# Scaling the residual rows on GpSimd in the up stages instead of the down stages, and two modulation vectors computed in the retention stage

## The chip, the core and the metric

One core of one Trainium2 chip runs the whole program. TensorE (PE) multiplies, VectorE (DVE), ScalarE (ACT) and GpSimd (POOL) do elementwise work, and the queue of SyncE (SP) issues most DMAs. Each engine works through its own instructions strictly in order and waits on semaphores for the others. The metric is device microseconds of one execution, taken as the median of several runs.

## The reference

Two layers, each a mixer and a convolutional feed-forward network (FFN), on 1024 rows of 1024 features in float32. The mixer of layer 0 is a gated delta net, that of layer 1 is retention. Cut to what the change touches:

```python
e = silu(c @ cond_w + cond_b)
for i in range(2):
    mod = e @ ada_w[i] + ada_b[i]
    sh1, sc1, g1, sh2, sc2, g2 = split(mod, 6)
    y = mixer[i](x * (1 + sc1) + sh1)
    x = layer_norm(ALPHA * x + (1 + g1) * y, ln_g[i, 0], ln_b[i, 0])
    y = conv_ffn(x * (1 + sc2) + sh2, ...)      # silu(conv(gate)) * up, then @ w_down
    x = layer_norm(ALPHA * x + (1 + g2) * y, ln_g[i, 1], ln_b[i, 1])
```

The six vectors of `mod` are numbered 0 to 5: groups 0 and 1 are `sh1` and `sc1`, 3 and 4 are `sh2` and `sc2`.

## The kernel before

**Matrix products.** The float32 operands are split in a rounded part and the rest (`split`, L88: ACT copies at L89, DVE subtracts at L90), and each product is three matmuls. The big products use a fast scheme with seven block products instead of eight. In `strassen` a function `wino(n, sink)` (L1207) handles item n: it loads two weight tiles `wa` and `wb` (1024 columns each, four blocks a11, a12, a21, a22; tag `wr`, two buffers, so the loads of an item wait until the item before has used its own), and computes seven products of 12 matmuls. Their left sides are a11, a12, and the sums s1, s2, s4, s3 that `psub` (L1204) has DVE write into PSUM tiles of the tag `mm` (two buffers), and a22. PE takes them in the order a11, a12, s1 (on T1), s2 (on T2), s4 (on 22), and then a22 (on T4) and s3 (on T3). `block` splits each left side into tiles `wb` first.

**Stages.** Layer 0: mixer, then the up product (22 items, two by two: an item for the convolved gate, an item for the up half; the results are stored in `ad`), then the down product (`proj_gen`). Layer 1: retention projections through `strassen` with 16 items, where items 0 and 1 and 10 to 15 make gates and items 2 to 9 are rope items (`rope_item`, L1610, with rotations on DVE and POOL), then the retention core, the output product, up and down as before. Items 0 and 1 of a `strassen` call are handled apart, `wino` takes the rest.

**Residual rows.** The layer norm that ends a mixer leaves rows without the gain and bias of the norm in `xs0` (layer 0) and `xs2` (layer 1). The down stage needs them with both, as float32 rows of the residual. `proj_gen` has POOL do this: `gain_half` (L1335) loads a 128x512 piece of rows 512 to 1023 into a `lane` tile, multiplies and adds (L1341), and stores it to `xg` (L1342) in the first two of the seven products; `xload` (L1344) loads rows 0 to 511 in the third product and scales them in place (L1349). Gain and bias are broadcast to all partitions by `gain_rows` into four tiles of the tag `auh` (eight buffers).

**Modulation vectors.** `bg_ada(i, j, kind)` queues eight units for one group of `mod`: each loads 512 KB of `ada_w` into a tile `mvw` (tag `lane`, four buffers, inside `strassen`) and has DVE multiply and add twice (L214, L216). The fourth and the eighth unit of a group also have PE transpose the 128x512 sum into an `mm` tile (L226), ACT sum it by rows (L228), and DVE add the bias (L230, L232). `wino` calls `bg_step` twice per item, and each call runs the next unit: once after the product on 22, once at the end of the item. The `mm` tile of the transposes thus comes from the same two buffers as the sums of `psub`.

**Order.** A scheduler turns the program's order into one order per engine; it may move an instruction ahead of others that it holds to be ready later.

Of the kernel before, what the change touches and what calls it, by code (L numbers as in the profile page):

```python
# [12 lines left out]
ALU = mybir.AluOpType  # L13
AX = mybir.AxisListType

P = 128
# [3 lines left out]
HALF = 512  # L20
# [13 lines left out]
def trunk_kernel(ctx: ExitStack, tc, A):  # L34
# [330 lines left out]
    def gain_rows(n, key, tag="auh"):  # L365
        return [row_load(A[nm][n:n + 1, :], key, sp, tag) for nm in ("ln_g", "ln_b")]
# [782 lines left out]
        dve.tensor_tensor(b, a, b, ALU.add)  # L1149
        return b  # L1150

    def strassen(hT0, xts, scale, shift, items, tags=("hTb", "hTb", "qkv", "qkv", "aux"), direct=False):
        B = {"11": hT0[:4], "21": hT0[4:]}
        nblk = [0]
        nacc = [0]

        def mm_on(*a, **kw):
            return pe.matmul(*a, skip_group_check=True, **kw)  # L1158
# [24 lines left out]

        def block(src):
            n = nblk[0]
            nblk[0] += 1
            t = tl(("wh", "wl")[n % 2], [P, 2, HALF], F32R, name="wb")
            split(t[:, 0], t[:, 1], src)
            return kn(t[:, 0]), kn(t[:, 1])

        def prod(src, b, onto=None):
            w = block(src)
            if onto is None:
                nacc[0] += 1
                acc = (acc_tile, acc_tile, sc_tile)[nacc[0] % 3]()
            else:
                acc = onto
            for k in range(4):
                mm3(acc, w, k, B[b][k], onto is None and k == 0, k == 3, mm_on if onto is not None else pe.matmul)
            return acc  # L1200

        def psub(x, y, op=ALU.subtract):
            t = mm_tile()
            dve.tensor_tensor(t, x, y, op)  # L1204
            return t

        def wino(n, sink):  # L1207
            ua, ub = items[n][:2]
            wa, wb = tl("wr", [P, D]), tl("wr", [P, D])
            sp.dma_start(wa, ua)  # L1210
            sp.dma_start(wb, ub)
            a11, a12, a21, a22 = wa[:, hs(0)], wa[:, hs(1)], wb[:, hs(0)], wb[:, hs(1)]
            def copy_of(X, tag="cv"):
                t = tl(tag, [P, 516] if tag == "cv" else [P, HALF], name="pc")[:, 0:HALF]
                act.activation(t, X, AF.Copy)  # L1215
                return t
# [12 lines left out]
            prod(s4, "22", Z)  # L1229
            sink(1, Z, u2)  # L1230
            bg_step()
            prod(s3, "T3", X)
            u3 = copy_of(X, "t2")
            sink(3, X, z5)
            sink(2, prod(a22, "T4"), u3)
            bg_step()

        bg_tag[0] = "lane"
        for n in range(2):
            if not direct:  # L1240
                sinks.append(items[n][2]())
                for i in range(2):
                    sinks[n](2 * i, ahead[n][i], None)
            X = side(n, 1)
            for i in range(2):
                sinks[n](2 * i + 1, X[i], None)
            if n == 0:
                rest()
            if items[n][3]:
                items[n][3]()  # L1250
        for n in range(2, len(items)):
            wino(n, items[n][2]())
            if items[n][3]:
                items[n][3]()
        bg_tag[0] = "wr"
        return B
# [5 lines left out]
            return raw  # L1262
        return ablk

    def proj_gen(nj, ablk, wsrc, slots, xsrc, G, final, ln_next, tag, ltags, dst, key, mm=pe.matmul, gate=None, gain=None):
# [64 lines left out]

        xts = [[], []]
        stats = [[], []]
        grows = gain_rows(gain[0], key) if gain else None

        def gain_half(n):  # L1335
            hf, rs = n // 4, slice(HALF + n % 4 * P, HALF + (n % 4 + 1) * P)
            x = tl("lane", [P, HALF], name="xg")
            with after("w"):
                sp.dma_start(x, gain[1][rs, hs(hf)])
            for r, op in zip(grows, (ALU.mult, ALU.add)):  # L1340
                pool.tensor_tensor(x, x, r[hf], op)  # L1341
            pool.dma_start(xsrc[rs, hs(hf)], x)  # L1342

        def xload(half, t):  # L1344
            xt = load_row(xsrc if half or not gain else gain[1], half, t)
            if half == 0 and gain:
                for r, op in zip(grows, (ALU.mult, ALU.add)):
                    for hf in range(2):
                        pool.tensor_tensor(xt[:, hs(hf)], xt[:, hs(hf)], r[hf], op)  # L1349
            xts[half].append(xt)  # L1350
            stats[half].append(tl("st", [P, 2, 6]))

        def finish(half, t, nh, c):
# [74 lines left out]
        for p, (an, bn, fin) in enumerate(prods):  # L1428
# [3 lines left out]
            for j in range(nj):  # L1432
                if gate and p < 2:
                    yield gate(j)
                    yield from take("qkv", 2)
                    give("qkv", 2)
                a, w = ops(an, bn, j, not gate and p < (7 if final else 5))
                with after("a"):
                    for st in steps[p * nj + j + ahead:p * nj + j + ahead + 1]:
                        load_b(*st)  # L1440
                if gain and p < 2 and j % 2 == 0 and p * 4 + j // 2 < 8 and j < 8:
                    gain_half(p * 4 + j // 2)
                if gain and p == 2 and j % 2 == 0 and j < 8:
                    xload(0, j // 2)
                if p == 2 and j < 4 and gate:
                    xload(0, j)
                    finish(0, j, 0, c11[j])
                if j >= nj - depth:
                    tail.append((j, a, w))
                else:  # L1450
                    for t in range(4):
                        mma(accs[t], t, a, w, j == 0, False, mm if p < 2 else pe.matmul)
                        yield 0.0
                if p == 5 and j > 1:
                    for _ in range(-(-16 // (nj - 2))):
                        if hooks:
                            hooks.pop(0)()
                bg_step()
# [27 lines left out]
    def layer_tail(i, mix, wout, xsrc, x_mid, x_out, ln_next, final):  # L1486
# [13 lines left out]
            hT0, xts = proj_st(mix[0])  # L1500
        bg_ada(i, 5, "row")
        if i == 0:
            for j in (1, 0, 4, 3):
                bg_ada(1, j, "col")
        cw = vcol(f"ffn_conv{i}")
        cb = vcol(f"ffn_convb{i}")
        ad = dr.tile([NF // 2, 7, P, HALF], F32, tag=f"ad{i}", name=f"ad{i}")
        up = A["ffn_up"][i]

        def pair_items(fp):  # L1510
            g, o = [], []
# [30 lines left out]
            def up_start():  # L1542
                seen = []

                def gated(q, a, b):
# [7 lines left out]
                    if len(seen) == 4:  # L1553
# [8 lines left out]
        strassen(hT0, xts, sc2, sh2, [it for fp in range(NF // 2) for it in pair_items(fp)])  # L1562
        slots = {"c": "hTa", "x": "qkv"}
        gb2 = gain_rows(3, ("mid", i), "hTb") if final else None
        return proj_st(proj_gen(NF // 2, ablk_of(ad, "qkv"), A["ffn_down"][i], slots, xg[i + 1], rows[i, 5],
                       (gb2, x_out) if final else None, ln_next, "hTb", ("hTb", "hTa", 8, 6, "f") if final else ("qkv", "hTa", 8, 4, "0"), x_out, ("out", i), gain=(2 * i, x_mid)))

    g1 = two("auh", F32, "g1")
    for nh in range(2):
# [64 lines left out]
    def gate_item(u):  # L1634
        def start():
            def sink(q, a, b):
# [4 lines left out]
        return A["ret_wg"][u], A["ret_wg"][u + 1], start, None  # L1641

    sc_r, sh_r = next0()
    B = strassen(h0, xts, sc_r, sh_r, [gate_item(0), gate_item(2)]
                 + [rope_item(h, j) for h in range(RH) for j in range(2)] + [gate_item(u) for u in range(4, 16, 2)], ("hTa", "aux", "qkv", "qkv", "hTa"), True)
    hT = [h0, []]
# [275 lines left out]
```

## Time and profile before

| | before |
|---|---|
| median of 3 runs | 3039.41 us (3034.10 to 3042.13) |
| profiled execution | 3032.61 us, of which its instructions span 3030.8 us |
| mean granted TensorE clock | 0.971 |
| up stage of layer 0, about | 840 to 1205 us of the span |
| down stage of layer 0, about | 1205 to 1480 us |
| rope items of retention, about | 1528 to 1690 us |
| up stage of layer 1, about | 2440 to 2790 us |
| down stage of layer 1, about | 2790 to 3030 us |
| POOL, L1341 (rows 512 to 1023) | 32 instructions, median 1629 ns, longest 17768 ns |
| SP loads at L210 (`ada_w`) | 80, median 4.3 us from issue to landing |

The trace is read by its views: the busy time of each engine in chosen stretches (with the granted clock of PE), the list of which engine waited for which, and the instructions in order of time. A row in order of time holds the start, the duration, engine, line, operation, output and input, size, and in brackets how long the engine had been idle and for what. Two rows that start 0.60 us apart and last 0.68 us overlap in the pipeline; the distance of the starts is then the cost of one. Consecutive matmuls overlap likewise.

### The profile page before, as it was taken

Reading aid. Unit: us, or ns where it says so; the run is one execution under the profiler, and the core shown is the slowest. Engines: PE = TensorE matmul, PEld = TensorE weight load, DVE = VectorE, ACT = ScalarE, POOL = GpSimd, SP = SyncE. Lnnn points to the kernel's source line nnn. Section 1 sums busy time; section 2 is a strip of 40 time slices with the busy share of each in tenths; the row PEclk is TensorE's granted clock in tenths of the full one; section 3 lists DMA queues with packets and bytes.
Section 4 is the critical chain, followed back from the end, with each engine's and each line's share of the span. In section 5 each row is a group of like instructions: output and inputs, shape, how many; then the busy total and the mean of one; then the engine's idle time right before and its main releaser. Section 6 shows DMA issues by size and latency. Waiting matters only on the chain. (4 is left out here: it accounts for less than half of the span.)

```text
span 3030.8 us, 38796 instructions
## 1 busy us (share of the span) xinstructions
PE 2840.2 (94%) x13590; PEld 2312.4 (76%) x13590; DVE 2271.4 (75%) x3841; ACT 1316.8 (43%) x2408; POOL 672.8 (22%) x629
## 2 busy tenths in 40 slices
PE   8889998999999999998999999999999899999997
PEld 7768876887778788786777787767777678888785
DVE  5785786545888888998788645566688887778988
ACT  4655555434544445445432442222243544445442
POOL 0410311033021111730023303422200011113704
PEclk9999998999999999999999999999998999999998
DMA  7222221354344545854322444666663332336663
GB/s 271 89 70 74 98 82 62 116 170 138 106 153 151 158 158 182 309 193 141 126 105 98 166 160 144 200 184 186 202 217 132 98 136 104 105 105 227 232 188 108
DMA packets 243027, 450.22 MB, mean 149 GB/s; under 512 B 22928, under 2 KB 76432, under 8 KB 242832
## 3 DMA queue, kind: packets, MB, share of 16 engines
q1 hardware_dynamic: 211648, 400.02, 40.0%
q10 hardware_dynamic: 29760, 43.00, 3.9%
q0 software_dynamic: 1424, 4.72, 0.4%
q8 instruction: 107, 1.75, 0.2%
q14 instruction: 88, 0.72, 0.1%
HBM read 339.13 MB, written 108.53 MB: 148 GB/s over the span
## 5 line engine op out<-in xcount | busy, mean ns | idle before, releaser
L636 PE MATMUL acc<-hT,wh 128*128 128x512 f32 x960 | 302.8, 397 | 0.0
L1556 POOL TENSOR_TENSOR o<-o 128x512 f32<-128x512 f32 x88 | 121.1, 1386 | 725.4 <-DVE o L1549 622.9
L279 PE MATMUL acc<-bb,ab 128*128 128x512 f32 x504 | 205.5, 408 | 18.8 <-DVE bb L90 18.7
L1158 PE MATMUL acc<-T,wb 128*128 128x512 f32 x840 | 205.3, 393 | 8.7 <-DVE wb L90 8.6
L636 PEld LDWEIGHTS acc<-hT,wh 128*128 128x128 f32 x960 | 184.3, 192 | 34.5
L278 PE MATMUL acc<-bb,ab 128*128 128x512 f32 x504 | 192.2, 407 | 16.9 <-DVE ab L90 10.3
L636 PE MATMUL acc<-hT,wl 128*128 128x512 f32 x480 | 204.3, 426 | 0.3 <-ACT sg L1084 0.3
L89 ACT ACTIVATE ab<-ar 128x512 fp32r<-128x512 f32 x210 | 129.8, 624 | 168.6 <-PE acc L280 87.9
L280 PE MATMUL acc<-bb,ab 128*128 128x512 f32 x504 | 202.6, 403 | 0.0
L1158 PEld LDWEIGHTS acc<-T,wb 128*128 128x128 f32 x840 | 157.9, 189 | 46.1 <-DVE wb L90 12.4
L90 DVE TENSOR_TENSOR wb<-wr,wb 128x512 fp32r<-128x512 f32 x162 | 116.0, 718 | 92.8 <-ACT wb L89 89.5
L90 DVE TENSOR_TENSOR ab<-ar,ab 128x512 fp32r<-128x512 f32 x210 | 169.2, 812 | 15.1 <-ACT ab L89 14.7
L90 DVE TENSOR_TENSOR wl<-wr,wh 128x1024 fp32r<-128x1024 f32 x85 | 106.4, 1252 | 89.7 <-ACT wh L89 89.7
L90 DVE TENSOR_TENSOR wb<-mm,wb 128x512 fp32r<-128x512 f32 x216 | 145.1, 683 | 22.8 <-ACT wb L89 20.9
L89 ACT ACTIVATE wh<-wr 128x1024 fp32r<-128x1024 f32 x101 | 106.8, 1058 | 121.3 <-PE acc L636 56.1
L89 ACT ACTIVATE wb<-mm 128x512 fp32r<-128x512 f32 x216 | 122.8, 593 | 72.5 <-DVE mm L1204 72.4
L1215 ACT ACTIVATE pc<-acc 128x512 f32<-128x512 f32 x143 | 84.5, 593 | 154.0 <-PE acc L1158 95.2
L636 PE MATMUL acc<-wh,hT 128*128 128x512 f32 x384 | 138.0, 422 | 2.0 <-DVE vv L90 2.0
L89 ACT ACTIVATE wb<-wr 128x512 fp32r<-128x512 f32 x162 | 99.3, 627 | 92.2 <-DMA wr<-in_ffn_up 45.9
L1535 DVE SCALAR_TENSOR_TENSOR o<-g,vc,o 128x512 f32<-128x512 f32 (+2 forms) x176 | 138.2, 804 | 0.8 <-ACT o L1530 0.2
L457 DVE SCALAR_TENSOR_TENSOR qkv<-raw,vc,qkv 128x512 f32<-128x512 f32 x144 | 114.6, 800 | 30.4 <-ACT qkv L455 29.3
L279 PEld LDWEIGHTS acc<-bb,ab 128*128 128x128 f32 x504 | 98.9, 196 | 44.7 <-DVE bb L90 24.3
(634 smaller groups left out, 7792.0 us busy)
## 6 DMA issues: line engine op xcount, KB each, us to landing
wr<-in_ffn_up SPq DMA_DIRECT2D x96, 512.0 KB, 4.0
mvw<-in_ada_w SPq DMA_DIRECT2D x80, 512.0 KB, 4.3
ad<-o SPq DMA_DIRECT2D x154, 256.0 KB, 2.2
ar<-ad SPq DMA_DIRECT2D x154, 256.0 KB, 4.4
Br<-in_ffn_down SPq DMA_DIRECT2D x88, 256.0 KB, 4.1
wr<-in_ret_wv SPq DMA_DIRECT2D x32, 512.0 KB, 3.7
ar<-od SPq DMA_DIRECT2D x56, 256.0 KB, 5.3
xs<-xt ACTq DMA_DIRECT2D x24, 512.0 KB, 3.8
```

The source lines that it names most:

```text
L89: act.activation(dst_h, src, AF.Copy)
L90: eng.tensor_tensor(dst_l, src, dst_h, ALU.subtract)
L278: mm(acc, a[1][:, sl], w[0], start=first, stop=False)
L279: mm(acc, a[0][:, sl], w[1], start=False, stop=False)
L280: mm(acc, a[0][:, sl], w[0], start=False, stop=last)
L457: dve.scalar_tensor_tensor(oh, raw[:, 3 - j:515 - j], w[:, 3 - j:4 - j], oh, ALU.mult, ALU.add)
L636: pq(pe.matmul(out, lhsT, rhs, start=start, stop=stop), cost)
L1158: return pe.matmul(*a, skip_group_check=True, **kw)
L1215: act.activation(t, X, AF.Copy)
L1535: dve.scalar_tensor_tensor(tv, gv[:, c0 - j:c1 - j], w[:, 2 - j:3 - j], tv, ALU.mult, ALU.add)
L1556: pool.tensor_tensor(o[d], o[x], o[y], op)
```

## The change

`gain_half` and the scaling in `xload` go. A new function `scale_rows` is called by `wino` right after the two weight loads of each item of an up stage. In item 5 it loads gain and bias; in each of items 6 to 21 it loads a 128x512 piece of the rows into an `auh` tile, has POOL multiply and add, and has POOL's queue store it to `xg`. All 1024 rows go that way, so the down stage loads finished rows. The order of the loads is pinned behind the load of `wb` (`anchor["i"]`).

In layer 0's `layer_tail`, groups 4 and 3 of layer 1 are no longer queued beside groups 1 and 0; they are queued ahead of the retention projections. There are two units per item and 16 units, so they fall on items 2 to 9, the rope items.

```diff
@@ wino
-            sp.dma_start(wb, ub)
+            anchor["i"] = sp.dma_start(wb, ub)
+            if beside:
+                beside(n)
@@ proj_gen
-        grows = gain_rows(gain[0], key) if gain else None
-
-        def gain_half(n):
-            hf, rs = n // 4, slice(HALF + n % 4 * P, HALF + (n % 4 + 1) * P)
-            x = tl("lane", [P, HALF], name="xg")
-            with after("w"):
-                sp.dma_start(x, gain[1][rs, hs(hf)])
-            for r, op in zip(grows, (ALU.mult, ALU.add)):
-                pool.tensor_tensor(x, x, r[hf], op)
-            pool.dma_start(xsrc[rs, hs(hf)], x)
-
         def xload(half, t):
-            xt = load_row(xsrc if half or not gain else gain[1], half, t)
-            if half == 0 and gain:
-                for r, op in zip(grows, (ALU.mult, ALU.add)):
-                    for hf in range(2):
-                        pool.tensor_tensor(xt[:, hs(hf)], xt[:, hs(hf)], r[hf], op)
-            xts[half].append(xt)
+            xts[half].append(load_row(xsrc, half, t))
...
-                if gain and p < 2 and j % 2 == 0 and p * 4 + j // 2 < 8 and j < 8:
-                    gain_half(p * 4 + j // 2)
-                if gain and p == 2 and j % 2 == 0 and j < 8:
+                if not gate and p == 2 and j % 2 == 0 and j < 8:
                     xload(0, j // 2)
@@ layer_tail
         if i == 0:
-            for j in (1, 0, 4, 3):
+            for j in (1, 0):
                 bg_ada(1, j, "col")
...
+        grows = []
+
+        def scale_rows(n):
+            if n == 5:
+                grows.extend(gain_rows(2 * i, "i"))
+            if not 6 <= n < 22:
+                return
+            hf, rs = (n - 6) // 8, slice((n - 6) % 8 * P, (n - 6) % 8 * P + P)
+            x = tl("auh", [P, HALF], name="xg")
+            with after("i"):
+                sp.dma_start(x, x_mid[rs, hs(hf)])
+            for w, op in zip(grows, (ALU.mult, ALU.add)):
+                pool.tensor_tensor(x, x, w[hf], op)
+            pool.dma_start(xg[i + 1][rs, hs(hf)], x)
@@ retention projections
     sc_r, sh_r = next0()
+    for j in (4, 3):
+        bg_ada(1, j, "col")
     B = strassen(h0, xts, sc_r, sh_r, ...
```

**POOL at the entry of the first down stage, before.** `o` are the up stage's last sums, `xg` the scaled pieces, `xt` whole rows of the residual.

```order
L1556 TENSOR_TENSOR o<-o 128x512 x40
L1341 TENSOR_TENSOR xg<-xg,rowb 128x512 x5
L1342 DMA xg_170<-xg 128x512 x2
L1341 TENSOR_TENSOR xg<-xg,rowb 128x512
L1342 DMA xg_170<-xg 128x512
L1556 TENSOR_TENSOR o<-o 128x512 x2
```

The same engine in the up stage of the change (its lines from 1211 on are numbered otherwise: L1555 is L1556 of before, L1506 and L1507 are new):

```order
L1555 TENSOR_TENSOR o<-o 128x512 x8
L1506 TENSOR_TENSOR xg<-xg,rowb 128x512 x2
L1507 DMA xg_170<-xg 128x512
L1555 TENSOR_TENSOR o<-o 128x512 x4
L1506 TENSOR_TENSOR xg<-xg,rowb 128x512 x2
L1507 DMA xg_170<-xg 128x512
```

One pair of POOL instructions and one store now stand in each item of the up stage from item 6 on, and the down stage has none.

**DVE at the start of a rope item, before.** `wb` are split halves of a block (L90), `mm` the sums of `psub` (L1204), `pc` and `rm` the values and products of the rotation (L1149, L1622 to L1627). The first row splits a11, the third makes s1, the fourth splits a12, and `wb_13504` is the split of s1.

```order
L90 TENSOR_TENSOR wb_13465<-wr_13461,wb_13465 128x512
L1149 TENSOR_TENSOR pc_13388<-acc_13356,pc_13388 128x512
L1204 TENSOR_TENSOR mm_13483<-wr_13462 128x512
L90 TENSOR_TENSOR wb_13485<-wr_13461,wb_13485 128x512
L1204 TENSOR_TENSOR mm_13502<-mm_13483,wr_13461 128x512
L1624 TENSOR_TENSOR pc_13388<-pc_13388,cosT_13268 128x512
L1149 TENSOR_TENSOR pc_13369<-sc_13317,pc_13369 128x512
L1149 TENSOR_TENSOR pc_13423<-sc_13438,pc_13423 128x512
L90 TENSOR_TENSOR wb_13504<-mm_13483,wb_13504 128x512
```

In the change, at the start of item 6 (items 4, 8 and 10 read alike), a12's split `wb_13754` is followed by eight rotation rows (cosine, two L1149, two products, difference, cosine, sum), and then by these; `ada` and `v14` belong to the modulation group, and `wb_13773` is the split of s1:

```order
L1625 TENSOR_TENSOR pc_13580<-pc_13580,rm_13706 128x512
L216 SCALAR_TENSOR_TENSOR ada_13498<-mvw_13715,e_162,ada_13498 128x512
L1149 TENSOR_TENSOR pc_13750<-acc_13757,pc_13750 128x512
L1626 TENSOR_TENSOR pc_13677<-pc_13677,rm_13706 128x512
L216 SCALAR_TENSOR_TENSOR ada_13498<-mvw_13715,e_162,ada_13498 128x512
L1204 TENSOR_TENSOR mm_13752<-wr_13731 128x512
L230 SCALAR_TENSOR_TENSOR v14_13388<-cs_13720,vc_153 128x4
L1204 TENSOR_TENSOR mm_13771<-mm_13752,wr_13730 128x512
L214 TENSOR_SCALAR ada_13828<-mvw_13829,e_162 128x512
```

Three small rows follow (L251, L252, L216), and then `wb_13773`. Before, s1 was made between the splits of a11 and a12; now it stands behind the whole rotation of the item before and behind the last unit of a modulation group, because that unit's transposes take an `mm` tile ahead of it in the program's order, and the split of s1 stands behind L230 and the first unit of the next group.

**SP in the rope items.** The `wr` are the two weight tiles of an item, the `mvw` the tiles of `ada_w`.

```order
L1210 DMA wr_13400<-in_ret_wqk 128x1024
L1211 DMA wr_13401<-in_ret_wqk 128x1024
L210 DMA mvw_13384<-in_ada_w 128x2x512
L210 DMA mvw_13499<-in_ada_w 128x2x512
L1794 DMA qk_15477<-qd_12622 128x512
```

Before, only `wr` (and now and then `qk`) stood there; two loads of 512 KB have moved in behind each pair of weight tiles. The tag `lane` of `mvw` also holds the products `rm` of the rotation and, all through retention, one table, so that a load of `mvw` can start only when an earlier `rm` or `mvw` is used up.

More of the change, by code (lines that the diff above doesn't have):

```diff
@@ L1150, in c_of, with strassen @@
         return b
-    def strassen(hT0, xts, scale, shift, items, tags=("hTb", "hTb", "qkv", "qkv", "aux"), direct=False):
+    def strassen(hT0, xts, scale, shift, items, tags=("hTb", "hTb", "qkv", "qkv", "aux"), direct=False, beside=None):
         B = {"11": hT0[:4], "21": hT0[4:]}
@@ L1263, in ablk_of, with proj_gen @@
         return ablk
-    def proj_gen(nj, ablk, wsrc, slots, xsrc, G, final, ln_next, tag, ltags, dst, key, mm=pe.matmul, gate=None, gain=None):
+    def proj_gen(nj, ablk, wsrc, slots, xsrc, G, final, ln_next, tag, ltags, dst, key, mm=pe.matmul, gate=None):
         bal = {nm: BAL[ltags[4] + nm] for nm in ABLK + ("w11", "w21", "w22", "wT1", "wT2", "wT3", "wT4", "n", "h")}
@@ L1560, in pair_items @@
             return [(up[4 * fp], up[4 * fp + 2], gate_start, conv), (up[4 * fp + 1], up[4 * fp + 3], up_start, None)]
-        strassen(hT0, xts, sc2, sh2, [it for fp in range(NF // 2) for it in pair_items(fp)])
+        strassen(hT0, xts, sc2, sh2, [it for fp in range(NF // 2) for it in pair_items(fp)], beside=scale_rows)
         slots = {"c": "hTa", "x": "qkv"}
@@ L1565, in layer_tail @@
         return proj_st(proj_gen(NF // 2, ablk_of(ad, "qkv"), A["ffn_down"][i], slots, xg[i + 1], rows[i, 5],
-                       (gb2, x_out) if final else None, ln_next, "hTb", ("hTb", "hTa", 8, 6, "f") if final else ("qkv", "hTa", 8, 4, "0"), x_out, ("out", i), gain=(2 * i, x_mid)))
+                       (gb2, x_out) if final else None, ln_next, "hTb", ("hTb", "hTa", 8, 6, "f") if final else ("qkv", "hTa", 8, 4, "0"), x_out, ("out", i)))
     g1 = two("auh", F32, "g1")
```

## The prediction

> **What bounds the kernel now.** First the totals, then the busy time by stage (stretch, length, busy us of PE, PEld, DVE, ACT and POOL with counts, granted clock, DMA share, GB/s), then the waits of PE (sum, times, longest).
>
> ```profile
> PE 2840.2 (94%) x13590; PEld 2312.4 (76%) x13590; DVE 2271.4 (75%) x3841; ACT 1316.8 (43%) x2408; POOL 672.8 (22%) x629
> ```
>
> PE is busy for 94% of the span and none of its matmuls goes away. So the time can change by PE's waits and by time at a lower granted clock, and by nothing else.
>
> ```profile
> 840.00:1205.00 365.00, 356.33 (x1559) 289.85 (x1559) 302.21 (x475) 167.66 (x331) 53.03 (x40) 1.00 0.48 156
> 1205.00:1410.00 205.00, 195.13 (x846) 158.17 (x845) 190.18 (x261) 99.29 (x180) 82.01 (x48) 0.98 0.70 238
> 1528.00:1690.00 162.00, 150.46 (x642) 121.59 (x642) 135.48 (x178) 48.87 (x85) 55.24 (x34) 0.98 0.32 111
> 2440.00:2790.00 350.00, 350.00 (x1543) 289.11 (x1542) 265.51 (x394) 166.39 (x283) 60.68 (x45) 1.00 0.37 127
> 2790.00:2940.00 150.00, 144.15 (x620) 118.15 (x619) 136.71 (x168) 66.14 (x118) 67.44 (x36) 0.98 0.67 229
> ```
>
> In order: up and the entry of down of layer 0, the rope items, up and the entry of down of layer 1. DVE is the runner-up everywhere: 93% in the first down stage, 91% in the second, 84% in the rope items, 83% and 76% in the up stages. The waits that end last are DVE's too, at the entry of down 0 (1205 to 1300), of down 1 (two rows), and in the rope items (two rows):
>
> ```profile
> PE acc L279 <- DVE bb L90: 5.0, 2, 3.6
> PE acc L279 <- DVE bb L90: 3.0, 1, 3.0
> PE acc L278 <- DVE ab L90: 2.9, 1, 2.9
> PE acc L1158 <- DVE wb L90: 7.5, 5, 2.6
> PE sc L1158 <- DVE wb L90: 4.1, 3, 2.6
> ```
>
> In up 1 no wait of PE is listed at all, as the equal 350.00 of length and PE's busy time says.
>
> **Part 1, the down stages lose their POOL work.** Why DVE is late there:
>
> ```profile
> 2803.60 5.97 DVE L90 TENSOR_TENSOR ab<-ar,ab 128x512 fp32r<-128x512 f32 x1
> 2809.49 0.68 DVE L90 TENSOR_TENSOR bb<-Bw,bb 128x512 fp32r<-128x512 f32 x1
> 2809.71 0.47 PE L278 MATMUL acc<-bb,ab 128*128 128x512 f32 x1 [2.86 <-DVE ab L90]
> ...
> 2841.50 10.99 DVE L1305 TENSOR_TENSOR Bw<-Bw 128x512 f32<-128x512 f32 x1
> 2841.93 10.01 POOL L1349 TENSOR_TENSOR xt<-xt,rowb 128x512 f32<-128x512 f32 x8
> 2853.15 0.50 PE L279 MATMUL acc<-bb,ab 128*128 128x512 f32 x1 [2.96 <-DVE bb L90]
> 2809.70:2814.70 5.00, 4.95 (x14) 3.75 (x15) 5.00 (x9) 0.66 (x2) 0.19 (x1) 0.66 0.95 311
> ```
>
> The same DVE subtract takes 0.68 us or 5.97, and one operation lasts 10.99 while eight POOL instructions (10.01) run beside it; 0.7 us after it ends, one split later, PE goes on. After such a stall the clock is granted at 0.66 for 5 us, which loses 5 x 0.34 = 1.7 us. Without POOL in these stages the four waits of L278 and L279 (5.0 + 3.0 + 2.9 = 10.9) and three such stretches (3 x 1.7 = 5.1) go: **-16**. At least the two long waits of down 1 and their last one's clock go (5.9 + 1.7, about -8); at most, with PE's other idle time in the row of 1205 to 1410 (205 - 195.1 - 5.0 = 4.9), about -21. Late next would be the loads, at 70% of the DMA in these rows; the change moves none of them in, and takes the loads of the pieces out.
>
> **Part 2, two modulation groups among the rope items.** The rows of the order show it: in items 4, 6, 8 and 10 the sum s1 comes after the whole rotation of the item before, after the last unit of a group and its transposes; the split of s1, without which PE can't start T1, also follows L230 and the next group's first unit (not in item 10, the last). PE holds two products then, a11 and a12. The rows for this walk:
>
> ```profile
> 1652.33 0.39 PE L110 MATMUL sc<-hT,wb 128*128 128x512 f32 x1
> 1657.77 0.39 PE L110 MATMUL acc<-T,wb 128*128 128x512 f32 x1
> 1654.90 1.27 DVE L1149 TENSOR_TENSOR pc<-acc,pc 128x512 f32<-128x512 f32 x2
> 1657.45 3.37 POOL L1625 TENSOR_TENSOR pc<-pc,cosT 128x512 f32<-128x512 f32 x2 [3.02 <-DVE rm L1622]
> 1662.50 1.28 DVE L90 TENSOR_TENSOR wb<-mm,wb 128x512 fp32r<-128x512 f32 x2
> 1663.23 4.62 PE L1158 MATMUL sc<-T,wb 128*128 128x512 f32 x12 [2.58 <-DVE wb L90]
> 1663.20:1668.20 5.00, 4.97 (x15) 3.94 (x16) 3.67 (x6) 2.03 (x4) 0.00 (x0) 0.66 0.67 210
> ```
>
> ```profile
> L214 DVE TENSOR_SCALAR ada<-mvw,e x20: 474/486/489, 72.3 to 2450.7; 128x512 f32<-128x512 f32 x20
> L216 DVE SCALAR_TENSOR_TENSOR ada<-mvw,e,ada x140: 710/745/1782, 73.3 to 2472.3; 128x512 f32<-128x512 f32 x140
> 1100.99 0.60 PE L226 MATMUL mm<-cst,ada 128*128 128x128 f32 x4
> 1224.32 0.26 ACT L228 ACTIVATE ada<-mm 128x128 f32<-128x128 f32 x1
> ...
> 1225.22 0.21 ACT L228 ACTIVATION_READ_ACCUMULATOR ada<-mm 128x1 f32 x1
> DMA to landing us min/median/max: 3.7/4.3/7.4
> ```
>
> Two products last 1657.77 - 1652.33 = 5.44 us. Say PE starts a11 at t. The last product of the item before ends at about t as well, and two of the rotation's inputs wait for it. From 1654.90 to 1662.50 DVE runs the eight rotation operations, one split and one sum, in 7.6 us; less 0.6 each for the last two, 6.4. Then two L216 (0.72 each, between the 0.71 and 0.745 of its row), L1149 and L1626 (0.6 each), 2.6: t + 9. Transposes 0.6: t + 9.6. The chain of L228 (1224.32 to 1225.43, four sums) and L230, 1.2: t + 10.8. s2 comes at t + 11.4, L214 (0.49) and L216 (0.72) bring t + 12.6, and the split of s1 0.6: t + 13.2. PE is through with a11 and a12 and the transposes at t + 5.44 + 0.6 = 6.0, so it idles for some 7.2, and 0.6 of the transposes is added work: **7.8** per item, and 6.6 in item 10, which lacks L214 and L216. Sum 3 x 7.8 + 6.6 = 30. If POOL (3.37 at 1657.45) stretches none of the eight operations (8 x 0.6 = 4.8 in place of 6.4), each is 1.6 less, sum 23.6. If a tile of `mvw` comes late (4.3 us median, 7.4 longest, the difference being 3.1), each is 3.1 more, sum 42.4.
>
> The clock comes on top:
>
> ```profile
> 473.60:486.00 12.40, 12.37 (x122) 10.23 (x124) 2.06 (x3) 7.28 (x14) 2.56 (x8) 0.51 0.12 40
> ```
>
> After the stall of 2.58 at 1663.23 it is 0.66 for 5 us, 1.7 lost; this longer row loses 12.4 x 0.49 = 6.1. I take 2.2 per item, near the short row since PE is dense on both sides: 9 (bounds 4 x 1.7 = 6.8 and 4 x 6.1 = 24).
>
> The Trainium skill ("TensorE: Matmul & The Clock Gate", section "What's actually happening") has PE at half rate after an idle window of about 3.4 us and at full rate after a busy one of as long. By that rule a stall of 7 us costs one window at half rate, an estimated 1.7, 7 in place of 9. The 0.66 over 5 us is 3.4 us at half rate, which fits; the row of 12.40 us at 0.51 doesn't, so I keep the larger value.
>
> On the other side stands what PE waits there already: 7.5 + 4.1 = 11.6 and two stretches at 0.66, 3.4, together 15, which the new order swallows. The other rope items keep about 2 (0 to 6). Net 30 + 9 + 2 - 15 = **+26**, bounds 23.6 + 6.8 + 0 - 15 = +15 and 42.4 + 24 + 6 - 15 = +57. SP's loads are covered: two of 512 KB per item more, in a stretch with a DMA share of 0.32. The sixteen units that leave up 0 and its down stage are 32 operations of DVE, 4 x 0.49 + 28 x 0.72 = 22 us, taken from a stretch in which PE waits little: nothing.
>
> **Part 3, the up stages gain 32 POOL operations each.** One pair per item from item 6. How such a pair meets DVE:
>
> ```profile
> 2638.08 2.99 POOL L1556 TENSOR_TENSOR o<-o 128x512 f32<-128x512 f32 x2 [0.15 <-POOL o L1556]
> 2638.25 0.68 DVE L1521 TENSOR_TENSOR g<-sc,pc 128x512 f32<-128x512 f32 x1
> 2638.85 1.08 DVE L1204 TENSOR_TENSOR mm<-wr 128x512 f32<-128x512 f32 x1
> 2639.84 1.77 DVE L1535 SCALAR_TENSOR_TENSOR o<-g,vc,o 128x511 f32<-128x511 f32 x1
> ...
> 1049.38 1.90 PE L1158 MATMUL acc<-T,wb 128*128 128x512 f32 x7 [0.48 <-DVE wb L90]
> ```
>
> In 2.99 us of POOL, L1521 with an input in PSUM keeps its 0.68, L1204 goes from 0.6 to 1.0, L1535 from 0.7 to 1.77, some 1.5 us of DVE. If all stretched like L1535, 2.99 us would hold 2.99 x 0.7 / 1.77 = 1.2 of work, 1.8 lost per pair. In up 1 DVE has 350 - 265.5 = 84 us free and PE never waits, so 16 x 1.8 = 29 find room: 0. In up 0 the items without slack are those after transposes, as at 1049.38, where PE waited 0.48; of those with a pair four keep their transposes (8, 10, 12, 14), 4 x 1.8 = 7.2, of which I take two thirds, since part of a pair falls on operations like L1521: **+5** (bounds 0 and +11, that is all of it and clock stretches of 1.7 in two of the four). POOL itself has room: 53 us busy of 365, plus 16 x 3.
>
> The Trainium skill ("SBUF — State Buffer", section "Who interferes with whom") lets a DVE instruction with two SBUF inputs and a GpSimd one lock each other out for a whole instruction, and spares one with at most one SBUF input. Here the sparing of L1521 agrees. By that rule only part of the up stages' operations stretch, and the sum of this part would be at or under 5.
>
> **Sum.** -16 + 26 + 5 = +15. On the profiled execution's own 3032.61 (of which 3030.8 is the span) that is 3047.6; the median of the runs is 6.8 higher, 3039.41, so the forecast is **3054**.
>
> **Rivals.** (1) Faster: the scheduler's order of the rope items costs no more than what PE waits there today, because the rotation, once ahead, frees DVE later in the item. The idle time at T1 must then stay under 15 / 4 = 3.75 us per item, clock included. The walk's sum of operations speaks against it, since DVE's queue alone is 13 us long; that the present 15 us are lost to the same rotation speaks for it. Then -16 + 0 + 5 = -11: 3028. (2) No change: the walk at its low end (POOL spares DVE, short clock stretches) and nothing lost in up: 15 + 0 - 16 = -1: 3038. For it speaks that POOL's pieces at 1657.45 cover only part of the eight operations. (3) Slower by more: up 0 pays in every item, 16 x 1.8 = 29 in place of 5: 3054 + 24 = 3078. Against it: 365 - 302 = 63 us of DVE are free there. (4) The change doesn't do what it says: POOL runs the pairs late, in the down stages, and part 1 is lost. In POOL's rows the pairs stand among the up stage's sums, and only the last is next to the stage's end.
>
> **How the numbers follow.** Forecast 0.64, (1) 0.12, (2) 0.17, (3) 0.06, (4) 0.01. A measurement tells 0.3%, about 9 us, from no change. So faster 0.12, same 0.18 from (2) and (4), slower 0.70. Low 3027, just under (1); high 3085: it takes in (3), and the forecast with 31 us more, which a late `mvw` in all four items (12) and two long clock stretches (2 x 3.9) and most of the other upper bounds make together; all upper bounds at once are left out.
>
> **What would show it.** Right: PE idle 6 to 9 us ahead of T1 in items 4, 6, 8 and 10, and shorter or no waits in the others; at the entry of both down stages no DVE operation over 2 us and no wait for `ab` or `bb`; in up 1 still no wait of PE; POOL's pairs spread over the up stages. Wrong: s1 made within 6 us of a11's start in the rope items, waits of PE for `wb` in most items of up 0, or waits of L278 and L279 that stay with POOL gone, so that loads were behind them.

## The result, and the profile after

The changed kernel takes 3075.08 us (median of 4 runs, 3071.40 to 3078.09); the kernel before took 3036.76 beside it. The ratio is 1.013, 95% interval 1.0109 to 1.0151: **slower by 38 us**. The forecast of 3054 had the sign, and its range of 3027 to 3085 held the time, but it had less than half of the loss. The ratio of rows_early below leaves out one execution of 7513 us, where its others took 3028 to 3043. The profiled execution took 3074.67 us, of which 3072.7 is the span, 41.9 more than before.

The totals of the changed kernel, then its busy time by stage (columns as in the prediction), in the stretches that hold the work of the rows shown of before: up and the entry of down of layer 0, the rope items, up and the entry of down of layer 1:

```profile
PE 2849.3 (93%) x13590; PEld 2318.8 (75%) x13590; DVE 2234.3 (73%) x3841; ACT 1315.9 (43%) x2408; POOL 637.1 (21%) x645
```

```profile
844.00:1214.00 370.00, 357.39 (x1559) 290.99 (x1558) 301.95 (x447) 166.31 (x309) 108.90 (x88) 1.00 0.48 163
1214.00:1418.00 204.00, 196.55 (x853) 160.82 (x853) 156.82 (x258) 101.83 (x177) 8.97 (x8) 0.97 0.62 210
1540.00:1738.00 198.00, 155.21 (x627) 123.78 (x626) 155.60 (x214) 51.97 (x116) 54.94 (x37) 0.88 0.42 135
2489.00:2839.00 350.00, 350.00 (x1540) 288.87 (x1539) 274.55 (x403) 164.52 (x282) 106.73 (x86) 1.00 0.44 153
2839.00:2979.00 140.00, 140.00 (x619) 115.96 (x618) 104.15 (x164) 65.73 (x116) 8.04 (x3) 1.00 0.65 217
```

The last two rows are as forecast: up 1 takes 46 us more of POOL and PE still never waits; down 1 has lost POOL, and PE is busy to the last microsecond. The third row is where the time went: PE is idle for 198 - 155 = 43 us among the rope items, at a mean clock of 0.88; before it was 162 - 150 = 12 us, at 0.98. The rope items' waits of PE (sum, times, longest):

```profile
PE mm L226 <- DVE ada L216: 19.7, 4, 5.0
PE acc L110 <- DVE wb L90: 8.3, 3, 3.8
PE sc L110 <- DVE wb L90: 7.5, 2, 3.8
PE sc L1158 <- DVE wb L90: 5.2, 2, 4.1
PE acc L1158 <- DVE wb L90: 2.1, 2, 1.1
```

The first row is four times the same: the transposes (L226) stand in PE's queue and wait for the modulation group's last sum (L216). L110 is the product on T1 behind them. Both executions run the same 13590 matmuls, so the starts of the same matmul can be subtracted, which tells the gain or loss of each stretch. The 16 transposes of the two moved groups stand in another place in some of the kernels, so they are left out on both sides before the matmuls are numbered. Worked out this way, against the profiled execution of before, in us (the first stretch ends in up 0 ahead of the first pair, where all kernels of this table run the same work; its 0.5 to 6.4 shows how well such a number, from one execution, repeats; the retention column ends with the rope items):

| kernel | ahead of the pairs | up 0 | its end and entry of down 0 | rest of down 0 | retention, to the end of the rope items | to up 1 | up 1 | entry of down 1 | rest |
|---|---|---|---|---|---|---|---|---|---|
| changed | 4.3 | 2.3 | -2.2 | -0.6 | 44.6 | 0.2 | 0.1 | -10.1 | 3.2 |
| rows_only | 1.0 | 5.7 | 1.8 | -0.6 | -0.2 | -2.7 | 0.4 | -10.1 | 0.1 |
| ada_only | 3.8 | -3.8 | -1.3 | 6.3 | 44.3 | 0.9 | -0.2 | -2.3 | 2.0 |
| ada_acc | 3.5 | 0.5 | -2.2 | -1.0 | 39.6 | 0.1 | -0.2 | -10.1 | 1.0 |
| ada_delay | 3.9 | 1.7 | -0.8 | 0.2 | 10.7 | -1.4 | 0.0 | -10.1 | 0.7 |
| ada_late | 2.5 | 0.8 | -6.8 | -2.1 | -1.0 | 13.6 | 2.2 | -10.1 | 1.2 |
| ada_notp | 6.4 | 1.4 | -1.9 | -1.4 | 3.3 | -0.1 | -0.1 | -10.1 | 0.8 |
| rows_early | 2.6 | 12.0 | -6.8 | -1.6 | -0.1 | -4.5 | 1.9 | -10.1 | 2.0 |
| rows_gbpool | 4.0 | 9.4 | -5.2 | -0.5 | -0.8 | -2.8 | 3.1 | -10.1 | 1.2 |
| rows_noscale | 0.5 | -1.6 | -4.5 | -0.9 | 0.1 | -2.5 | 2.5 | -10.1 | 1.1 |
| rows_l1 | 0.6 | -0.3 | 1.0 | 0.0 | 0.1 | -2.9 | 1.0 | -10.1 | -1.9 |

### The profile page after: what moved, and what is told of

It is laid out like the page before. It is cut to its first block, busy times and chain, and to the rows that moved or that the text cites. A ratio compares the mean times of both kernels' runs of the same rounds, so it can differ in the third digit from the quotient of the medians.

```text
span 3072.7 us, 38818 instructions
## 1 busy us (share of the span) xinstructions
PE 2849.3 (93%) x13590; PEld 2318.8 (75%) x13590; DVE 2234.3 (73%) x3841; ACT 1315.9 (43%) x2408; POOL 637.1 (21%) x645
## 4 chain that ended last, share of the span: by engine, by line
PE 58%; DVE 21%; DMA 10%; issue 5%; ACT 4%; POOL 2%; SPq 0%; POOLq 0%; DVEq 0%; ACTq 0%
PE acc L636 14%; PE acc L1158 6%; PE sc L1158 4%; PE acc L110 3%; PE sc L636 3%; PE acc L111 3%; PE acc L112 3%; PE acc L279 3%; PE acc L280 3%; PE acc L278 3%; DMA wr<-in_ffn_up 2%; DVE o L1534 2%; PE mm L636 2%; DVE wb L90 2%; DMA mvw<-in_ada_w 2%
## 5 line engine op out<-in xcount | busy, mean ns | idle before, releaser
L279 PE MATMUL acc<-bb,ab 128*128 128x512 f32 x504 | 202.1, 401 | 11.7 <-DVE bb L90 11.6
L1158 PE MATMUL acc<-T,wb 128*128 128x512 f32 x840 | 203.6, 391 | 4.5 <-DVE wb L90 4.2
L278 PE MATMUL acc<-bb,ab 128*128 128x512 f32 x504 | 189.3, 401 | 13.6 <-DVE xt L1342 7.8
L90 DVE TENSOR_TENSOR ab<-ar,ab 128x512 fp32r<-128x512 f32 x210 | 151.7, 727 | 67.9 <-ACT ab L89 67.7
L280 PE MATMUL acc<-bb,ab 128*128 128x512 f32 x504 | 200.2, 399 | 0.0
L90 DVE TENSOR_TENSOR wb<-wr,wb 128x512 fp32r<-128x512 f32 x162 | 120.8, 748 | 97.5 <-ACT wb L89 97.0
L1158 PEld LDWEIGHTS acc<-T,wb 128*128 128x128 f32 x840 | 157.0, 188 | 40.8 <-DVE wb L90 7.3
L1555 POOL TENSOR_TENSOR o<-o 128x512 f32<-128x512 f32 x88 | 126.2, 1445 | 266.7 <-DVE o L1548 154.2
L1506 POOL TENSOR_TENSOR xg<-xg,rowb 128x512 f32<-128x512 f32 x64 | 91.4, 1428 | 424.0 <-DMA xg<-xs 421.5
L90 DVE TENSOR_TENSOR wl<-wr,wh 128x1024 fp32r<-128x1024 f32 x85 | 106.3, 1250 | 92.6 <-ACT wh L89 92.6
L90 DVE TENSOR_TENSOR wb<-mm,wb 128x512 fp32r<-128x512 f32 x216 | 144.9, 683 | 26.8 <-ACT wb L89 25.7
L1534 DVE SCALAR_TENSOR_TENSOR o<-g,vc,o 128x512 f32<-128x512 f32 (+2 forms) x176 | 156.8, 913 | 0.6
```

What stands on the lines that cost most here:

```text
L90: eng.tensor_tensor(dst_l, src, dst_h, ALU.subtract)
L278: mm(acc, a[1][:, sl], w[0], start=first, stop=False)
L279: mm(acc, a[0][:, sl], w[1], start=False, stop=False)
L280: mm(acc, a[0][:, sl], w[0], start=False, stop=last)
L1534: dve.scalar_tensor_tensor(tv, gv[:, c0 - j:c1 - j], w[:, 2 - j:3 - j], tv, ALU.mult, ALU.add)
L1555: pool.tensor_tensor(o[d], o[x], o[y], op)
```

## The experiments

### The two parts apart

**rows_only** keeps the groups in up 0:

```diff
-            for j in (1, 0):
+            for j in (1, 0, 4, 3):
                 bg_ada(1, j, "col")
...
-    for j in (4, 3):
-        bg_ada(1, j, "col")
```

> The change without its move of the two modulation groups: they stay in the up stage of layer 0, the rows are scaled by GpSimd in both up stages. Theory A (the two parts add up, and the loss is the groups' alone): retention as before; down 1 about -11, entry of down 0 about -7, up 0 +5 to +9: together -13 to -5 us, some 3028, ratio 0.996 to 0.998. Theory B (the pairs in up cost much more as long as all five modulation groups stand there too): up 0 pays in most items, 16 x 1.8 = 29, and the whole is slower than before by 5 to 15 us.

Measured: 3030.10 us, ratio 0.9997 (0.9982 to 1.0012). **ada_only** is the kernel before with the opposite edit, the groups moved and the rows scaled in down:

> The kernel before with the move of the two groups alone; rows are scaled in the down stages as before. Theory A: the rope items cost +41 us as in the changed kernel, up 0 gains 0 to 3, down 0 gains 0 to 5 from six DVE operations less: 3070 to 3080, ratio 1.010 to 1.014. Theory B (the loss needs both parts together): under +20 us.

Measured: 3081.41 us, ratio 1.0167 (1.0143 to 1.0190), a little more than expected. By the table the parts add up where they act: retention loses 44.3 with the groups' move alone and nothing without it; down 1 gains 10.1 wherever layer 1's rows are scaled in up; up 0 pays 5.7 for the pairs and gains 3.8 from the groups that leave it, and 2.3 is what the changed kernel shows. The whole doesn't add up as well: the two ratios together make 1.0164, some 10 us over the changed kernel's 1.0130. In the table the rest of down 0 of ada_only loses 6.3 where a gain was expected; PE waits there once for 6.2 us (L278 for DVE's split `ab`), in a down stage where POOL still scales rows. And rows_only gains less than its -13 to -5. Its up 0 costs 5.7, as expected, and the end of up 0 with the entry of down 0 gives +1.8 in place of -7.

### What holds PE in the rope items

First item 6 of the changed kernel. The chain that ended last, in order of time, from the end of the item before to PE's transposes (start, length, what):

```profile
1611.81 2.73 PE acc L1158 x12
1614.54 0.02 issue
1614.56 0.61 ACT pc L1217
1615.17 0.02 issue
1615.19 1.29 DVE pc L1149 x2
1616.48 1.20 DVE rm L1621 x2
1617.68 1.70 DVE pc L1625
1619.38 1.68 DVE pc L1623
...
1624.13 0.67 DVE ada L216
1624.80 0.14 issue
1624.94 1.10 PE mm L226 x4
```

And the same item in order of time, behind the transposes:

```profile
1614.36 0.39 PE L110 MATMUL sc<-hT,wb 128*128 128x512 f32 x1
...
1624.94 1.08 PE L226 MATMUL mm<-cst,ada 128*128 128x128 f32 x4 [4.97 <-DVE ada L216]
...
1627.23 0.16 DVE L230 SCALAR_TENSOR_TENSOR v<-cs,vc 128x4 f32<-128x4 f32 x1 [1.83 <-ACT ada L228]
...
1629.12 0.68 DVE L90 TENSOR_TENSOR wb<-mm,wb 128x512 fp32r<-128x512 f32 x1
...
1629.86 0.80 PE L110 MATMUL acc<-T,wb 128*128 128x512 f32 x1 [3.84 <-DVE wb L90]
```

PE starts a11 at 1614.36 and T1 only at 1629.86, 15.5 us later, with 5.4 us of products and 1.1 of transposes between; PE idles for 4.97 + 3.84 = 8.8 of them, where the prediction named 6 to 9 as its sign. The route is the prediction's: end of the product on T4, rotation, last sums of the group, transposes, L228, split of s1. Whether the `mm` tiles or something else ties it together, the next four kernels tell.

**ada_acc** takes the PSUM tile of the transposes from another tag, so that s1 no longer waits for one:

```diff
-            bg_step()
+            bg_step(acc_tile if direct else mm_tile)
```

(the same at both calls of an item)

> The changed kernel, but in the retention projections the transposes of a group go into a PSUM tile of the tag acc in place of one of mm; the work is the same to the instruction. Theory A (the loss is s1's place behind the transposes, by way of the two mm tiles): the two stalls of 5.3 and 4.2 us in items 4, 6, 8 and 10 and their half clock shrink to 1 to 3 us per item: 3032 to 3045, 30 to 43 us less than the changed kernel. Theory B (it is the amount: 32 operations and 22 us more on DVE, sixteen loads more): within 10 us of the changed kernel.

Measured: 3064.59 us, ratio 1.0111 (1.0088 to 1.0135), retention +39.6. In its order s1 is indeed made ahead of most of the rotation again. Theory A fell all the same; the number is the one of theory B, but the rows name another cause. In order of time:

```profile
1668.29 0.74 DVE L216 SCALAR_TENSOR_TENSOR ada<-mvw,e,ada 128x512 f32<-128x512 f32 x1
1669.09 0.71 PEld L226 LDWEIGHTS acc<-cst,ada 128*128 128x128 f32 x4 [10.35 <-DVE ada L216]
1669.09 1.12 PE L226 MATMUL acc<-cst,ada 128*128 128x128 f32 x4 [9.93 <-DVE ada L216]
```

s1 is ready (its split starts at 1660.09), but PE works in order, and the transposes stand ahead of it: PE waits for L216 itself, once for 9.9 us. That gives a third theory, A': not the tile, but the place of the transposes in PE's order, right behind a sum that DVE makes after the rotation. **ada_delay** issues the same transposes half an item later (`tail` is the transposes, their sums and the bias; a step runs what is left over first):

```diff
     def bg_step(tile=mm_tile):
         bg_ps[0] = tile
+        if pend:
+            pend.pop(0)()
...
+                if bg_late[0]:
+                    pend.append(tail)
                 else:
+                    tail()
```

> The changed kernel, but in the retention projections the transposes of a finished half group, with the sums and the bias behind them, are issued one half item later, behind the next item's product on 22. The same instructions in another place. Theory A' (the loss is the place of the transposes in PE's order: PE stands at them until the last L216 is done, which DVE does after the rotation): the four stalls of 9 us go, items keep 1 to 3 us each: 3035 to 3050. Theory B (the amount of work on DVE and in the loads): 3060 or more, with waits of PE for wb in every rope item.

Measured: 3033.36 us, ratio 1.0008 (0.9995 to 1.0021), 2 us under the range of A'. The stalls at the transposes are gone. PE's waits among its rope items (L1167 is L1158 of the others):

```profile
PE acc L1167 <- DVE wb L90: 8.6, 5, 2.4
PE sc L1167 <- DVE wb L90: 8.1, 3, 4.0
PE acc L110 <- DVE wb L90: 1.1, 1, 1.1
```

With every load and every DVE operation of the groups still in the rope items, retention costs 10.7 in place of 44.6: **34 us are the place of the transposes** and of the sums and the bias that hang on them. **ada_late** moves the units instead, past the rope items:

```diff
+    bg.extend([lambda: None] * 16)
     for j in (4, 3):
         bg_ada(1, j, "col")
```

> The changed kernel, but with sixteen empty steps ahead of the two groups, so that their units fall on the gate items 10 to 15 and the last four units on the steps after the projections. Theory A' : gate items have no rotation, the last L216 is early, and stalls are 0 to 2 us: 3030 to 3045. Theory B: DVE is free for more than half of the gate items (56 us busy in 120), so it has the same sign here, and only ada_delay tells the two apart; above 3055 would speak against both and for the loads.

Measured: 3032.93 us, ratio 0.9998 (0.9987 to 1.0010). The rope items are as before, and the transposes, now in the gate items and just behind them, have no wait of PE, as A' has it. But 13.6 is lost between the rope items and up 1, half of it in the gate items, where most of the units now run; whether they are its cause was not pursued. **ada_notp** leaves out the transposes, their sums and the added bias, so its result lacks them:

```diff
+                if i == 1 and j in (3, 4):
+                    dve.tensor_add(v, b, b)
+                    return
```

> The changed kernel without the transposes, their sums and the added bias for groups 4 and 3 of layer 1 (their vectors are twice the bias then): the sixteen units load, multiply and add as in the changed kernel. Theory A': the four stalls go, what is left is DVE's 32 operations, 1 to 2 us per item: 3035 to 3045. Theory B: within 15 us of the changed kernel.

Measured: 3025.54 us, ratio 0.998 (0.9966 to 0.9994), 10 us under the low end of A'. Its matmuls are 4.6 us behind before at the start of the retention stretch and 7.8 at its end (the same matmuls, transposes left out on both sides). PE's waits among its rope items (L1161 is L1158 of the others):

```profile
PE acc L1161 <- DVE wb L90: 8.2, 5, 1.7
PE sc L1161 <- DVE wb L90: 7.4, 3, 4.1
```

So the amount, theory B, costs some 3 us there: of the 44.6, 34 are the transposes' place behind the late sum, and another 7 go with the transposes, of which 2.4 are their own time on PE (16 x 0.15). The 3 is a single execution's number and no surer than the first column of the table; for the 7 the medians say the same, with ada_notp 7.8 us under ada_delay on one chip.

### The end of up 0

rows_only loses what it gains there, in one stall:

```profile
PE sc L1158 <- DVE wb L90: 5.9, 1, 5.9
```

Its rows in order of time, SP's queue (SPq) and DVE:

```profile
1206.51 0.33 SPq L377 DMA_DIRECT2D gb<-in_ln_g  x1
1210.56 0.33 SPq L377 DMA_DIRECT2D gb<-in_ln_b  x1
1210.94 1.45 SPq L210 DMA_DIRECT2D mvw<-in_ada_w  x3
...
1217.11 0.75 DVE L216 SCALAR_TENSOR_TENSOR ada<-mvw,e,ada 128x512 f32<-128x512 f32 x1 [4.87 <-DMA mvw<-in_ada_w]
```

L377 loads a gain and a bias for a later task into tiles of `auh`, the tag in which the change keeps its pieces. SP stands at the second load for 4 us, and the loads of `ada_w` behind it are late for L216; a split that PE needs is behind L216 on DVE. In the changed kernel the same two loads hold up the first loads of down, and ACT, which stands at one of them, has a copy for PE behind it:

```profile
1204.48 0.33 SPq L377 DMA_DIRECT2D gb<-in_ln_g  x1
1204.75 0.59 POOL L1507 DMA_DIRECT2D xg<-xg  x1 [0.30 <-POOL xg L1506]
...
1208.46 0.33 SPq L377 DMA_DIRECT2D gb<-in_ln_b  x1
1208.88 1.33 SPq L1296 DMA_DIRECT2D Bw<-in_ffn_down  x3
...
1217.01 0.63 ACT L89 ACTIVATE ab<-ar 128x512 fp32r<-128x512 f32 x1 [3.33 <-DMA ar<-ad]
...
1219.21 0.50 PE L1158 MATMUL acc<-22_7032,wb 128*128 128x512 f32 x1 [3.65 <-ACT pc L1217]
```

The second load starts 3.7 us after the store of the last piece (L1507) is issued. In before no piece lies in this tag, and no load at L377 stands at the end of up 0. **rows_early** moves the pairs two items ahead (`n == 3`, items 4 to 19):

> The kernel rows_only with the pairs in items 4 to 19 in place of 6 to 21. Theory S (the stall of 6.3 us at the end of up 0 comes from SP: two loads at L377 wait for a buffer of auh that the last scaled piece holds until its store has landed, and the loads of the down stage and of ada_w stand behind them): that stall goes, with its clock stretch 6 to 9 us less than rows_only, some 3022. Rival (it is DVE's and POOL's load in the last items): within 3 us of rows_only.

Measured: 3035.41 us, ratio 1.0005 (0.9991 to 1.0019): no gain, as the rival has it. But the rows don't speak for the rival. The stall did not go, it went along: the scheduler put L377 behind the last piece again, two items earlier. Two rows from its lists of waits and of SP's instructions:

```profile
PE acc L1158 <- DVE wb L90: 4.8, 1, 4.8
```

```profile
1171.10 0.33 SPq L377 DMA_DIRECT2D gb<-in_ln_b  x1
1171.48 1.45 SPq L210 DMA_DIRECT2D mvw<-in_ada_w  x3
```

So the wait follows the loads, not the place in the program. **rows_gbpool** takes them off SP:

```diff
-                    sp.dma_start(t, A[nm][n:n + 1, hs(c)].to_broadcast([P, HALF]))
+                    pool.dma_start(t, A[nm][n:n + 1, hs(c)].to_broadcast([P, HALF]))
```

> The kernel rows_only with the two loads at L377 issued by POOL's queue in place of SP's; they stand behind the last scaled piece there as well. Theory S (SP stands at these two loads until the last pieces are stored, and the loads behind them come late): PE's wait of 5.9 us at the end of up 0 and its stretch at half clock go, up 0 to the first down rows 6 to 9 us shorter than in rows_only, whole time 0.996 to 0.998 of before. Rival (the loads of the down stage and of ada_w are late for another reason, or the wait is DVE's own): a wait of 4 us or more stays at the end of up 0.

Measured: 3029.14 us, ratio 0.998 (0.9967 to 0.9994). PE's waits from 1190 to 1240:

```profile
PE acc L278 <- DVE ab L90: 0.8, 1, 0.8
PE acc L110 <- DVE wb L90: 0.7, 1, 0.7
PE sc L1158 <- DVE wb L90: 0.3, 1, 0.3
```

The stall is gone, as theory S says, and the entry of down 0 now gains 5.2. The wait itself is now seen on POOL's queue, and it ends with the landing of the last store:

```profile
1218.39 0.55 POOL L377 DMA_DIRECT2D gb<-in_ln_b  x1 [4.59 <-DMA xg<-xg]
```

But the way to the first down rows is only 3.3 us shorter than in rows_only, not 6 to 9: up 0 pays 9.4 in this profile, 3.7 more than there, with 14 waits of up to 1.0 us (900 to 1190), 9.1 in all; why more than there was not pursued.

### What the pairs cost in up 0, and the best version

**rows_noscale** drops POOL's 32 operations in up 0, so that layer 0's rows lack gain and bias:

```diff
-            for w, op in zip(grows, (ALU.mult, ALU.add)):
+            for w, op in zip(grows if i else [], (ALU.mult, ALU.add)):
```

> The kernel rows_only without POOL's 32 multiplications and additions in the up stage of layer 0 (its rows are loaded and stored without gain and bias). Theory P (up 0 pays some 8 us because POOL's pairs stretch DVE's operations in items without slack): waits of PE of 1.0 to 1.4 us in its items shrink to before's 0.5 to 0.9 and up 0 ahead of its end is within 2 us of before. Rival (the sixteen loads and stores, or the order that the scheduler makes, cost it): the waits stay. By Theory S the stall at the end shrinks only by as much as the last piece is stored earlier, 3 us, and 2 to 6 us of it stay.

Measured: 3017.51 us, ratio 0.9947 (0.9928 to 0.9965). PE's only wait on DVE from 900 to 1240 is then the one at the end, as forecast:

```profile
PE sc L1158 <- DVE wb L90: 2.2, 1, 2.2
```

Up 0 falls from +5.7 to -1.6: POOL's pairs cost 7 us of PE there. In rows_only PE waited ten times between 900 and 1200, up to 1.0 us each and 7.0 in all; without the pairs none of these waits is left. **rows_l1** scales in up in layer 1 alone (`beside=scale_rows if i else None`, and the old path in layer 0):

> The kernel before, with the rows scaled in the up stage in layer 1 alone; layer 0 and the modulation groups as before. Theory A (up 1 has room for all 16 pairs, and POOL's work is what stalls down 1): up 1 within 1 us, down 1 -11: 3026, ratio 0.996 to 0.997. Rival: the gain of down 1 belongs to something else of the change (the order there, loads that come earlier), or up 1 pays once layer 0 is undisturbed: within 4 us of before.

Measured: 3020.61 us, ratio 0.9969 (0.9954 to 0.9984). Its entry of down 1:

```profile
2780.00:2930.00 150.00, 150.00 (x664) 124.19 (x663) 113.73 (x178) 70.83 (x125) 9.69 (x4) 1.00 0.66 229
```

**rows_l1b**, the same kernel again:

> The kernel rows_l1 once more, beside rows_gbpool on one chip. Theory: down 1's gain of some 10 us with nothing on the other side, 0.995 to 0.998 of before. If rows_gbpool's layer 0 gains as much in down as it loses in up, the two are within 5 us of each other; if rows_gbpool is over 5 us faster, the scaling pays in layer 0 too.

Measured: 3021.60 us, ratio 0.9972 (0.9958 to 0.9986). It is the best of the kernels that compute the whole: some 9 us, 0.3%, faster than before. rows_gbpool, beside it, is 7.5 us slower by the medians and 5.4 by the means, a little more than the 5 us of the expectation. So the scaling in layer 0 takes more in up than it gives in down, even with the two loads off SP; the table has 9.4 against 5.2.

## Why the forecast had the sign and not the size

The profiled executions differ by 41.9 where the sum had 15. By the table, part 2 came as 44.6 in place of 26, part 1 as -12.3 in place of -16, and up 0 as 2.3 in place of 5. Another 7.5 stand in the first and the last stretch, for which nothing was forecast; the work of the first is the same in both kernels. **The step that failed is the sum of part 2**: its four stalls were taken 10 us too short, and its term for the other rope items, "about 2 (0 to 6)", came as 12.

**Part 1, the down stages: right for layer 1, with a neighbour overlooked in layer 0.** Down 1 gained 10.1 at its entry in every kernel with the scaling moved, against 9.3 forecast for it (5.9, and two of the three clock stretches); the waits for `ab` and `bb` went there, and the operations of 5.97 and 10.99 us are gone from DVE. No kernel here moves POOL's work without the loads of the pieces, so that POOL and not the loads made these waits is read from the rows of before, where the operation of 10.99 runs beside POOL's 10.01. Down 0's entry gains 5 to 7 where nothing else disturbs it (rows_early, rows_gbpool). What failed is the step "the change moves none of them in": no load was moved into down 0, but the change put its pieces into a tag from which SP fetches tiles for a later task, and SP's queue then stood still ahead of down's first loads. In the changed kernel this took back about 5 (-2.2 against rows_early's -6.8), of which PE's wait of 3.65 at L1158 is shown above.

**Part 2, the rope items: the route right, two terms mis-sized.** The time from one a11 to the next, in us; an item without a wait takes 19.0 (item 11, both kernels):

| item | 3 | 4 | 5 | 6 | 7 | 8 | 9 | 10 |
|---|---|---|---|---|---|---|---|---|
| before | 19.5 | 20.4 | 20.3 | 20.7 | 20.6 | 21.0 | 23.5 | 23.5 |
| changed | 27.2 | 31.1 | 20.4 | 31.0 | 20.4 | 30.8 | 20.4 | 30.8 |
| ada_delay | 25.0 | 22.6 | 21.1 | 21.5 | 23.3 | 21.4 | 23.3 | 21.6 |

- The four stalls, forecast 30. The walk had T1 at 13.2 us after a11's start, item 6 has 15.5. The walk's clock started at t, but the first rotation operation waits for ACT's copy of the T4 product and starts at 1615.19, 0.8 late; the eight operations took 7.0 (1615.19 to 1622.19) in place of 6.4; the transposes and L228 took 2.3 (1624.94 to 1627.23) in place of 1.8. With 15.5 - 5.4 = 10.1 for each of the four, and item 10 no cheaper (9.9), it is **40 in place of 30**.
- The clock, forecast 9. What the four items took over 19.0 beyond these stalls is some 8, so it was about right. Its row in item 4:

```profile
1572.20:1582.40 10.20, 5.21 (x14) 3.97 (x15) 6.90 (x13) 3.42 (x12) 0.00 (x0) 0.50 0.46 153
```

- The other items, "about 2 (0 to 6)". Items 5, 7 and 9 took 1.4 each over 19.0, item 3 took 8.2: **12 in place of 2**. In item 3 PE waits once for 4.1, and the clock is at half for 6.8 us around it. Item 3 takes 24.2 to 25.2 in ada_delay, ada_late and ada_notp too, whose units differ, and 19.7 in rows_only; what makes it stays open.
- What before lost in the same eight items, forecast 15, is 17. Sum 40 + 8 + 12 - 17 = 43; the remaining 2 of the 44.6 came ahead of item 3.
- What the groups' leaving gives in up 0 was put at nothing, because PE waits little there; by ada_only it is 3.8 in up 0 and 1.3 at its end.

The explanation was also narrower than it was told. The prediction laid the stall on s1, which waits for an `mm` tile behind the transposes. ada_acc freed s1 and won 5 of 44.6; ada_delay, which moves the transposes and so frees s1 from them as well, won 34. So the place of the transposes in PE's order is enough for most of the loss; what s1's place alone would cost, with the transposes out of PE's way, no kernel here tells.

Of the rivals, the low end of the walk (2) is excluded by the 40 us, and so is (1). The number of (3), 3078, is nearest to the measured 3075, by luck: it laid the loss on up 0 at 29 us, where the pairs cost 5.7 in rows_only.

**Part 3, the up stages: right.** The pairs cost up 0 5.7 in rows_only, 5 forecast; up 1 nothing, 0 forecast. In the changed kernel up 0 shows only 2.3, since the groups left it. rows_noscale shows that it is POOL's operations which cost it. The Trainium skill ("SBUF — State Buffer", section "Who interferes with whom") has an operation of DVE with two SBUF inputs and one of GpSimd exclude each other; the waits that vanish with the 32 POOL operations agree.

## What to carry to other kernels

Background work with a piece on the busiest in-order engine is priced by where that piece stands, not by its length: two groups with 2.4 us of transposes cost 45 us, 34 of which were gone once the transposes stood half an item further behind the sum that another engine makes for them. A new tile is priced with its tag's other users: whoever fetches the next tile from that tag may stand at the head of a queue that others need. And a change with two parts is taken apart by layer as well: the same move paid 10 us in the layer whose up stage had room and cost 4 to 8 in the other (up 0 and the entry of down 0 of rows_only, rows_early and rows_gbpool). When two executions are compared matmul by matmul, what stands in another place is left out first: 16 transposes more or fewer shift every matmul between their two places by some 3.6 us (0.23 each).

## What was not expected of the hardware

The granted clock stayed at half for 10.2 us around two stalls of 5.0 and 3.8 us with 1.1 us of work between them, while a single stall of 2.6 us before had 0.66 over 5 us, that is 3.4 us at half rate. The Trainium skill ("TensorE: Matmul & The Clock Gate", section "What's actually happening") gives windows of 3413 ns; 10.2 us is three of them (3 x 3.413), so the little work between the stalls did not bring the clock back. The stall of 2.6 us, shorter than one such window, was enough for a stretch at half rate. Four stretches of 10.2 us lie around the four double stalls, each from within the first wait to some 4 us after the second.
